# Delta-rule chain in full 128x128 matmuls: z computed beside y1, one block-diagonal inverse for two heads, state columns beside y2

## The chip, the cores and the metric

The kernel runs on one core of one Trainium2 chip. The metric is the device time of one execution in microseconds; of several executions the median is taken. Engines are named as the profile names them: PE (TensorE, matrix multiplication), PEld (its weight loads), DVE (VectorE), ACT (ScalarE), POOL (GpSimd) and SP (SyncE, which issues the DMAs).

## The reference, cut to what matters

The reference is one decoder block on 512 tokens of width 1024: an RMS norm, two parallel token mixers (HGRN2 with 8 heads, RWKV-7 with 16 heads of 64), a gated merge and output projection, and a gated convolutional feed-forward part. The change is in the RWKV-7 mixer, a delta rule whose state has 64 x 64 entries per head:

```
def step(state, inp):
    r_t, w_t, k_t, v_t, a_t, b_t = inp
    sa = jnp.einsum('bhvk,bhk->bhv', state, a_t)
    state = (state * w_t[:, :, None, :] + sa[..., None] * b_t[:, :, None, :]
             + v_t[..., None] * k_t[:, :, None, :])
    y = jnp.einsum('bhvk,bhk->bhv', state, r_t)
    return state, y
```

Its output y is normalised per head, scaled, joined by a bonus term and a gate, and projected.

## The kernel before, in words

**Stages.** A first phase projects the normalised input by the 66 column blocks of `w_in` (128 columns each) and runs both mixers. The second phase multiplies both mixers' outputs by `w_branch_a` and `w_branch_b` (tile `yps`, line 1223), merges, projects by `w_out`, and runs the feed-forward part. The large products are done as three float32r matmuls each (high and low parts of both operands); every weight block is loaded by SP into `raw`, its high part is cast on ACT (`whi_t`), its low part subtracted on POOL (`wlo_t`). The mixers' own products are fp32 matmuls; each fp32 matmul is two PE instructions in the trace.

**The delta rule in chunks.** The 16 heads are treated as 8 pairs (`hb`), one head in partitions 0 to 63 (`hs[0]`), the other in 64 to 127 (`hs[1]`). The 512 tokens are cut into NCH = 8 chunks of 64. For each pair there are three generators:
- `front` (line 702) prepares decayed keys and queries (`gt`, `bk`), multiplies them into the chunk's score matrices (`sc`), masks these into `lr` (strictly lower part for the inverse, lower part with diagonal for y2) and `gt`, and transposes `bk` into `bkn`. All lie in `X`, a buffer of which there are two; so front of pair hb waits for `("chain", hb - 2)` at line 746, and its first step behind that wait is `kka` (line 750).
- `solve` (line 817) inverts each chunk's unit triangular 64 x 64 matrix in blocks of 16, with two DMA round trips, into `Q` (a 64 x 64 inverse per head, each in its head's partitions).
- `chain` (line 872) steps through the 8 chunks. `sv` holds, per chunk and head, the state in the head's own partitions and the values in the other head's. A step first computes z (lines 887 to 889) and y1 (890 to 893), from `gt` and `sv`, with outputs in half of the partitions each; copies z to `zs` on DVE (895); multiplies by the inverse (902); scales the result into `sv` on DVE, once per head (905); computes the state update from `bkn` (908) and y2 from `lr` (910), which adds to y1 in PSUM (`yp`); and adds the decayed state `sp` (made on ACT, 900) into the next chunk's `sv` on DVE, once per head (918). Behind the last step stands a part that normalises `yp` (its first instruction is the reduction into `ym`, 926), transposes it and writes it out. chain of pair hb starts when solve of pair hb and all of chain of pair hb - 1 are through.

A chain step has ten matmuls (eight in the last chunk): four for z and y1, two by the inverse, two for the state, two for y2. Their stationary operands are 64 columns wide. PE forms in the profile give the array's rows and columns in use, as in `128*64`, and then the moving operand.

**The order of the work.** In the first phase every engine's instructions are put in a fixed order by a planner (class `Plan`, line 78). Generators yield one operation at a time; the planner prices each (`cost`, line 152), computes when its operands are ready (`prepare`, line 129: end of the producer plus a hop, and `MARGIN` = 0.6 us more for PE), and emits the operation that can start first, with a head start (`BONUS`) for the chain. On the chip each engine runs its list in that order. Dense products fill PE between the rest: `load`, `splits` and `gemm` (lines 1089, 1106, 1144) handle one weight block each, with gates: a block is loaded when the pair it feeds has got far enough. The blocks of the two merge gates come last: GA is let go at `("late", 6)`, GB at `("late", 7)`, which chain sets behind its sixth chunk (line 919). The second phase begins when they are done.

## Time and profile before

| | |
|---|---|
| median of 3 runs | 1256.02 us (1255.92 to 1258.85) |
| the profiled execution | 1255.5 us, its span 1253.8 us |
| granted TensorE clock over the span | 0.989 |
| PE busy | 1210.6 us (97%), 7748 matmul instructions |
| DVE, ACT, POOL busy | 732.7, 463.6, 536.0 us |
| first phase | from the start to 743.7 us |
| first chain's first z, last chain's last y2 | 153.2 us, 682.1 us |

The time of an execution is its span and what lies around it. A row of the timeline gives start, duration, engine, line, operation, output tile and input tiles, the PE form, and how many like instructions were merged; 207 is the line of the planner's `emit`, so in the first phase instructions are told apart by their tiles: `us<-sv,X` is z and the state update, `yp<-sv,X` y1 and y2, `us<-zs,Q` the product with the inverse, `zps` a dense product. Matmul durations overlap; what one costs PE is the distance from its start to the next one's.

### The profile page before, as it was taken

How to read it: one execution, taken by the hardware profiler on the slowest of the kernel's cores; microseconds unless marked ns; L12 is line 12 of the kernel's file. 1: busy time of each engine (PE TensorE's matmuls, PEld its weight loads, DVE VectorE, ACT ScalarE, POOL GpSimd, SP SyncE). 2: the span in 40 equal slices, each digit the busy share in tenths (PEclk: the TensorE clock that was granted, in tenths of full speed). 3: DMA queues.
4: the chain of work that ended last, by engine and by line, in shares of the span. 5: the costliest groups of instructions: out<-in, count | busy, mean ns of one | idle time of the engine just before them, and what ended most of it. 6: DMA issues, size and time to landing. Idle time of an engine off the chain costs nothing.

```text
span 1253.8 us, 19765 instructions
## 1 busy us (share of the span) xinstructions
PE 1210.6 (97%) x7748; PEld 949.7 (76%) x7748; DVE 732.7 (58%) x1563; ACT 463.6 (37%) x825; POOL 536.0 (43%) x420
## 2 busy tenths in 40 slices
PE   8889999999999999999999999999999999999997
PEld 6667668667668677686767888888988888888886
DVE  6988887787888988886746304335523232322213
ACT  5533334333343443343332532225534343342321
POOL 6444224342332423242424454432466575565631
PEclk9889899999999999999999999999999999999999
DMA  5121212112112122121221733254323232232332
GB/s 178 50 68 58 65 43 87 49 55 68 50 61 64 54 65 68 43 75 55 70 72 49 240 118 118 86 186 156 130 85 115 90 112 84 84 101 80 122 101 84
DMA packets 54061, 111.01 MB, mean 89 GB/s; under 512 B 21584, under 2 KB 24784, under 8 KB 53968
## 3 DMA queue, kind: packets, MB, share of 16 engines
q1 hardware_dynamic: 53968, 109.75, 27.6%
q8 instruction: 61, 1.00, 0.3%
q14 instruction: 32, 0.26, 0.1%
HBM read 100.29 MB, written 9.44 MB: 88 GB/s over the span
## 4 chain that ended last, share of the span: by engine, by line
PE 75%; DVE 15%; issue 3%; ACT 3%; POOL 2%; DMA 1%; SPq 0%; DVEq 0%; POOLq 0%; ACTq 0%
PE zps L207 20%; PE zps L323 6%; PE zps L322 6%; PE zps L321 6%; PE dn L321 3%; PE dn L323 3%; PE dn L322 3%; PE us L207 3%; PE sc L207 2%; PE yps L321 2%; PE yps L323 2%; PE yps L322 2%; PE vps L207 2%; PE mix L207 2%; DVE X L207 2%
## 5 line engine op out<-in xcount | busy, mean ns | idle before, releaser
L207 POOL TENSOR_TENSOR wlo_t<-raw,whi_t 128x512 fp32r<-128x512 f32 x134 | 184.6, 1397 | 351.3 <-ACT whi_t L207 319.8
L279 POOL TENSOR_TENSOR wlo_t<-raw,whi_t 128x1024 fp32r<-128x1024 f32 x80 | 194.6, 2439 | 96.4 <-ACT whi_t L279 96.2
L207 PE MATMUL zps<-xl,whi_t 128*128 128x512 f32 x488 | 201.3, 413 | 0.0
L207 PE MATMUL zps<-xh,wlo_t 128*128 128x512 f32 x488 | 201.2, 412 | 0.0
L207 PE MATMUL zps<-xh,whi_t 128*128 128x512 f32 x488 | 200.6, 411 | 0.0
L279 ACT CAST whi_t<-raw 128x1024 fp32r<-128x1024 f32 x80 | 83.3, 1049 | 175.5 <-DMA raw<-wup 64.5
L1378 DVE SCALAR_TENSOR_TENSOR u<-zps,pr,u 128x511 f32<-128x511 f32 x40 | 30.0, 750 | 190.7 <-ACT u L1377 190.7
L207 ACT CAST whi_t<-raw 128x1024 fp32r<-128x1024 f32 x71 | 74.4, 1048 | 147.1 <-PE zps L207 68.1
L321 PE MATMUL zps<-x2h,whi_t 128*128 128x512 f32 x320 | 125.5, 392 | 0.0
L323 PE MATMUL zps<-x2h,wlo_t 128*128 128x512 f32 x320 | 125.5, 392 | 0.0
L322 PE MATMUL zps<-x2l,whi_t 128*128 128x512 f32 x320 | 125.5, 392 | 0.0
L207 PEld LDWEIGHTS zps<-xl,whi_t 128*128 128x128 f32 x488 | 92.5, 190 | 20.6 <-issue 0.5
L207 PEld LDWEIGHTS zps<-xh,wlo_t 128*128 128x128 f32 x488 | 92.7, 190 | 20.1 <-issue 0.2
L207 PEld LDWEIGHTS zps<-xh,whi_t 128*128 128x128 f32 x488 | 92.8, 190 | 19.4 <-issue 0.2
L321 PEld LDWEIGHTS zps<-x2h,whi_t 128*128 128x128 f32 x320 | 60.2, 188 | 13.5
L322 PEld LDWEIGHTS zps<-x2l,whi_t 128*128 128x128 f32 x320 | 60.2, 188 | 13.5
L323 PEld LDWEIGHTS zps<-x2h,wlo_t 128*128 128x128 f32 x320 | 60.1, 188 | 13.4
L1403 POOL TENSOR_TENSOR th<-th,u 128x512 f32<-128x512 f32 x22 | 28.4, 1292 | 71.2 <-DVE u L1379 71.2
L207 ACT ACTIVATE sp<-sv,pel 64x64 f32<-64x64 f32 x96 | 33.0, 344 | 67.0 <-DVE sv L207 65.8
L207 PEld LDWEIGHTS us<-sv,X 128*64 128x64 f32 (+1 forms) x480 | 23.8, 134 | 39.7 <-issue 11.6
L207 DVE TENSOR_SCALAR sv<-us,rn 64x64 f32<-64x64 f32 x128 | 35.8, 280 | 29.0 <-PE us L207 25.3
L321 PE MATMUL yps<-oh,whi_t 128*128 128x512 f32 x128 | 50.2, 392 | 0.0
(375 smaller groups left out, 2601.0 us busy)
## 6 DMA issues: line engine op xcount, KB each, us to landing
raw<-win SPq DMA_DIRECT2D x64, 512.0 KB, 3.7
raw<-wup SPq DMA_DIRECT2D x44, 512.0 KB, 3.5
raw<-wdn SPq DMA_DIRECT2D x22, 512.0 KB, 3.5
raw<-wbr SPq DMA_DIRECT2D x16, 512.0 KB, 3.4
raw<-whi SPq DMA_DIRECT2D x8, 512.0 KB, 3.5
raw<-wout SPq DMA_DIRECT2D x8, 512.0 KB, 3.5
xt<-xT SPq DMA_DIRECT2D x8, 256.0 KB, 6.4
oa_d<-hg SPq DMA_DIRECT2D x8, 256.0 KB, 2.2
```

What stands on the lines that cost most here:

```text
L207: op.ins_ = self.seq(op.key, op.fn(*op.args, **op.kw))
L279: return A.copy(hi, raw), eng.tensor_tensor(lo, raw, hi.bitcast(F32), op=ALU.subtract)
L321: T.matmul(o, lh, rh, start=start, stop=False)
L322: T.matmul(o, lh, rl, start=False, stop=False)
L323: T.matmul(o, ll, rh, start=False, stop=stop)
L1378: V.scalar_tensor_tensor(u[:, 1:S], ps[:, 0 : S - 1], pc("cw1", b), u[:, 1:S], op0=ALU.mult, op1=ALU.add)
L1403: G.tensor_tensor(th, th, uv_, op=ALU.mult)
```

## The change

- **z beside y1.** `gt` holds both operands side by side, so one matmul with 128 stationary columns per head gives z in one half of the output's partitions and y1 in the other. In chunk 0 it now runs over all 128 rows, and the empty half of `sv` is zeroed on POOL.
- **One inverse for both heads.** Two tiles `qd` (128 x 128 per chunk, zeroed once each) hold the two inverses as diagonal blocks; a single matmul serves both heads. `solve` still works in a tile `Q` (now one buffer) and copies the halves into `qd` on ACT.
- **State columns beside y2.** `lr` and `bkn` become `w2`: per chunk and head 128 columns, of which the head's own 64 hold `bkn` and the other 64 the y2 scores in the head's rows. In the other head's rows these 64 columns first hold the strictly lower part for `solve`, which zeroes them on POOL when it is through. One matmul per head gives the state update and y2, in the last chunk too.
- **y.** y1 and y2 no longer add up in PSUM. ACT copies each, per head and chunk, into `ys` and `yb`; DVE adds the two once per pair. z goes to `zs` half on DVE, half on ACT, and of the two scalings of `sv` one goes to ACT.
- **PSUM.** Five 64-column slots per step wander through 16 slots in two banks (`ua`, `ub`).
- **Room and planner.** `sgx` has one buffer, `f2` is gone (the scan of `p2` runs in place), `fm` uses `Tn`, `qs` overwrites `qi`. The planner prices a matmul of 64 moving by 128 stationary columns at 0.112 us.

Per chain step: matmuls ten to five, all in the form 128*128; DVE copies, scalings and additions five to four; ACT operations two to eight.

```
+            elif n == 64 and m == 128:
+                op.us = 0.112
...
+    qds = [mx.tile([P, NCH, P], F32, name=f"qd{i}") for i in range(2)]
...
-        lr = X[:, 4 * S : 6 * S].rearrange("p (n x c) -> p n x c", n=NCH, x=2)
-        bkn = X[:, 6 * S : 8 * S].rearrange("p (n c) -> p n c", n=NCH)
+        w2 = X[:, 4 * S : 8 * S].rearrange("p (n h c) -> p n h c", n=NCH, h=2)
...
-                yield V1.tensor_tensor(lr[q, n0 : n0 + 4, h], sc[q, :, h], mr[q, n0 : n0 + 4], op=ALU.mult)
-                yield V1.tensor_tensor(lr[q, n0 : n0 + 4, 1 - h], sc[q, :, 1 - h],
+                yield V1.tensor_tensor(w2[q, n0 : n0 + 4, 1 - h, hs[h]], sc[q, :, h], mr[q, n0 : n0 + 4], op=ALU.mult)
+                yield V1.tensor_tensor(w2[q, n0 : n0 + 4, h, hs[1 - h]], sc[q, :, 1 - h],
...
-            yield A1.copy(bkn[:, 4 * half : 4 * half + 4], tp)
+            dst = w2[:, 4 * half : 4 * half + 4].rearrange("p n h c -> p n (h c)")
+            dst = bass.AP(dst.tensor, dst.offset, [list(dst.ap[0]), [2 * P, 4], [P + 64, 2], [1, 64]])
+            yield A1.copy(dst, tp.rearrange("p n (h c) -> p n h c", h=2))
...
-        Q = mx.tile([P, NCH, 64], F32, name="Q", bufs=2)
+        Q = mx.tile([P, NCH, 64], F32, name="Q")
+        qd = qds[hb % 2]
+        if hb < 2:
+            yield G1.memset(qd, 0.0)
...
-        fm = mx.tile([P, NCH, 64], F32, name="fm")
+        fm = Tn
...
         yield V1.tensor_tensor(Q, Q, dps, op=ALU.add)
+        for h in range(2):
+            yield A1.copy(qd[hs[h], :, hs[h]], Q[hs[h]])
...
-            yield A1.copy(Q[a, :, 32:64], dps2[a])
+            yield A1.copy(qd[a, :, 64 * h + 32 : 64 * h + 64], dps2[a])
+        for h in range(2):
+            yield G1.memset(w2[hs[h], :, 1 - h, hs[h]], 0.0)
...
         sv = mx.tile([P, NCH, 2, 64], F32, name="sv")
+        for h in range(2):
+            yield G1.memset(sv[hs[h], 0, h], 0.0)
...
-        yp = pyz.tile([P, NCH, 64], F32, name="yp")
-        us = pus.tile([P, 8, 64], F32, name="us", tag="us")
+        ua = pus.tile([P, 8, 64], F32, name="us", tag="us")
+        ub = pyz.tile([P, 8, 64], F32, name="yp")
+        ys = mx.tile([P, NCH, 64], F32, name="ys")
+        yb = mx.tile([P, NCH, 64], F32, name="yb")
+
+        def slot(i):
+            return (ua if i % 16 < 8 else ub)[:, i % 8]
+
         for n in range(NCH):
-            zslot, uslot, sslot = (3 * n) % 8, (3 * n + 1) % 8, (3 * n + 2) % 8
-            for h in (1, 0):
-                kp = slice(0, P) if n > 0 else hs[1 - h]
-                yield T1.matmul(us[hs[h], zslot], gt[kp, n, h, h], sv[kp, n, h], start=True, stop=True)
-            for h in (1, 0):
-                kp = slice(0, P) if n > 0 else hs[1 - h]
-                yield T1.matmul(yp[hs[1 - h], n], gt[kp, n, h, 1 - h], sv[kp, n, h], start=True, stop=False,
-                                skip_group_check=True)
+            zy, us, sy = [slot(5 * n), slot(5 * n + 1)], slot(5 * n + 2), [slot(5 * n + 3), slot(5 * n + 4)]
+            for h in range(2):
+                yield T1.matmul(zy[h], gt[:, n, h].rearrange("p x c -> p (x c)"), sv[:, n, h], start=True, stop=True)
             zs = small.tile([P, 64], F32, name="zs")
-            yield V1.tensor_copy(zs, us[:, zslot])
+            yield V1.tensor_copy(zs[hs[0]], zy[0][hs[0]])
+            yield A1.copy(zs[hs[1]], zy[1][hs[1]])
...
-            for h in (1, 0):
-                yield T1.matmul(us[hs[h], uslot], Q[hs[h], n], zs[hs[h]], start=True, stop=True)
             for h in range(2):
-                q = hs[h]
-                yield V1.tensor_scalar(sv[q, n, h], us[q, uslot], rn2[q, n : n + 1], None, op0=ALU.mult)
-            if n < NCH - 1:
-                for h in (1, 0):
-                    yield T1.matmul(us[hs[h], sslot], bkn[:, n, hs[h]], sv[:, n, h], start=True, stop=True)
-            for h in (1, 0):
-                yield T1.matmul(yp[hs[1 - h], n], lr[hs[h], n, 1 - h], sv[hs[h], n, h], start=False, stop=True,
-                                skip_group_check=True)
+                yield A1.copy(ys[hs[1 - h], n], zy[h][hs[1 - h]])
+            yield T1.matmul(us, qd[:, n], zs, start=True, stop=True)
+            yield V1.tensor_scalar(sv[hs[0], n, 0], us[hs[0]], rn2[hs[0], n : n + 1], None, op0=ALU.mult)
+            yield A1.activation(sv[hs[1], n, 1], us[hs[1]], AF.Identity, scale=rn2[hs[1], n : n + 1])
+            for h in range(2):
+                yield T1.matmul(sy[h], w2[:, n, h], sv[:, n, h], start=True, stop=True)
             if n < NCH - 1:
...
+            for h in range(2):
+                yield A1.copy(yb[hs[1 - h], n], sy[h][hs[1 - h]])
...
-        ys = mx.tile([P, NCH, 64], F32, name="ys")
+        yield V1.tensor_tensor(ys, ys, yb, op=ALU.add)
...
-        yield V1.tensor_tensor_scan(p2.rearrange("p a n c -> p (a n c)"), f2.rearrange("p a n c -> p (a n c)"),
+        yield V1.tensor_tensor_scan(p2.rearrange("p a n c -> p (a n c)"), p2.rearrange("p a n c -> p (a n c)"),
```

More of the change, by code (lines that the diff above doesn't have):

```diff
@@ L391, in block_kernel @@
     Gi.memset(mh, 1.0)
-    sgx = [pers.tile([P, NCH, 65], F32, name=f"sgx{i}") for i in range(2)]
+    sgx = pers.tile([P, NCH, 65], F32, name="sgx")
     m65 = pers.tile([P, NCH, 65], F32, name="m65")
@@ L400, in block_kernel @@
     scm = pers.tile([P, NT, P], F32, name="scm")
-    for t_ in sgx:
-        Gi.memset(t_[:, :, 0:1], 0.0)
-    Gi.memset(f2[:, :, :, 0:1], 0.0)
+    Gi.memset(sgx[:, :, 0:1], 0.0)
     Gi.memset(scm, 0.0)
@@ L715, in front @@
         yield T1.matmul(wps, lw[:, 0:P], zws, start=False, stop=True)
-        sg = sgx[hb % 2]
+        sg = sgx
         yield A1.activation(sg[:, :, 1:65], c8(wps), AF.Tanh, scale=0.5, bias=hw0[:, hb : hb + 1])
@@ L796, in front @@
                 yield D1.dma_start(lb_d[:, h, b].rearrange("n s t -> s n t"),
-                                   lr[p0 : p0 + 16, :, h, 16 * b : 16 * b + 16])
-        st_[hb] = [vt[hb], gt, lr, bkn, pel, rn2]
+                                   w2[p0 : p0 + 16, :, 1 - h, p0 : p0 + 16])
+        st_[hb] = [vt[hb], gt, w2, pel, rn2]
         fin.add(("lb", hb))
-        plan.spawn("solve", solve(hb, lb_d, lr))
+        plan.spawn("solve", solve(hb, lb_d, w2))
         bks = bk.rearrange("p n x c -> p n (x c)")
@@ L813, in front, with solve @@
                 yield T1.transpose(tp[:, n], bks[:, 4 * half + n], ident)
-            yield A1.copy(bkn[:, 4 * half : 4 * half + 4], tp)
+            dst = w2[:, 4 * half : 4 * half + 4].rearrange("p n h c -> p n (h c)")
+            dst = bass.AP(dst.tensor, dst.offset, [list(dst.ap[0]), [2 * P, 4], [P + 64, 2], [1, 64]])
+            yield A1.copy(dst, tp.rearrange("p n (h c) -> p n h c", h=2))
         fin.add(("front", hb))
-    def solve(hb, lb_d, lr):
+    def solve(hb, lb_d, w2):
         if hb > 0:
@@ L841, in solve @@
             for h in range(2):
-                yield T1.matmul(fps[hs[h], n], lr[hs[h], n, h], Tn[hs[h], n], start=True, stop=True)
-        fm = mx.tile([P, NCH, 64], F32, name="fm")
+                yield T1.matmul(fps[hs[h], n], w2[hs[h], n, 1 - h, hs[h]], Tn[hs[h], n], start=True, stop=True)
+        fm = Tn
         yield V1.tensor_tensor(fm, fps, mf.unsqueeze(1).broadcast_to([P, NCH, 64]), op=ALU.mult)
@@ L855, in solve @@
             for n in range(NCH):
-                yield T1.matmul(fps2[b, n], lr[a, n, h, 32:64], Tn[a, n, 0:32], start=True, stop=True)
+                yield T1.matmul(fps2[b, n], w2[a, n, 1 - h, b], Tn[a, n, 0:32], start=True, stop=True)
         for h in range(2):
@@ L866, in solve @@
             a = slice(64 * h, 64 * h + 32)
-            yield A1.copy(Q[a, :, 32:64], dps2[a])
+            yield A1.copy(qd[a, :, 64 * h + 32 : 64 * h + 64], dps2[a])
+        for h in range(2):
+            yield G1.memset(w2[hs[h], :, 1 - h, hs[h]], 0.0)
         yield done(("front", hb))
-        st_[hb].append(Q)
+        st_[hb].append(qd)
         fin.add(("solve", hb))
     def chain(hb):
-        v, gt, lr, bkn, pel, rn2, bo, Q = st_.pop(hb)
+        v, gt, w2, pel, rn2, bo, qd = st_.pop(hb)
         sv = mx.tile([P, NCH, 2, 64], F32, name="sv")
+        for h in range(2):
+            yield G1.memset(sv[hs[h], 0, h], 0.0)
         vp = pus.tile([P, NT, P], F32, name="vp", tag="us")
@@ L915, in chain @@
                     if n == 0:
-                        yield V1.tensor_copy(sv[q, 1, h], us[q, sslot])
+                        yield V1.tensor_copy(sv[q, 1, h], sy[h][q])
                     else:
-                        yield V1.tensor_tensor(sv[q, n + 1, h], us[q, sslot], sp[h][q], op=ALU.add)
+                        yield V1.tensor_tensor(sv[q, n + 1, h], sy[h][q], sp[h][q], op=ALU.add)
+            for h in range(2):
+                yield A1.copy(yb[hs[1 - h], n], sy[h][hs[1 - h]])
             if n == NCH - 3:
@@ L923, in chain @@
         yield D1.dma_start(lgr, wlg[hb, :, 2 * P : 3 * P])
-        ys = mx.tile([P, NCH, 64], F32, name="ys")
+        yield V1.tensor_tensor(ys, ys, yb, op=ALU.add)
         ym = small.tile([P, NCH], F32, name="ym")
-        yield V1.tensor_reduce(ym, yp, axis=AX.X, op=ALU.add)
+        yield V1.tensor_reduce(ym, ys, axis=AX.X, op=ALU.add)
         yield V1.tensor_single_scalar(ym, ym, 1.0 / 64, op=ALU.mult)
-        yield V1.tensor_tensor(ys, yp, ym.unsqueeze(2).broadcast_to([P, NCH, 64]), op=ALU.subtract)
-        yield A1.activation(yp, ys, AF.Square)
+        yield V1.tensor_tensor(ys, ys, ym.unsqueeze(2).broadcast_to([P, NCH, 64]), op=ALU.subtract)
+        yield A1.activation(yb, ys, AF.Square)
         yss = small.tile([P, NCH], F32, name="yss")
-        yield V1.tensor_reduce(yss, yp, axis=AX.X, op=ALU.add)
+        yield V1.tensor_reduce(yss, yb, axis=AX.X, op=ALU.add)
         yield from rsq1(yss, NCH, 64 * GN_EPS)
@@ L1041, in hgrn @@
             yield T1.matmul(ups[:, t], k3[:, t], vn[:, t, hv], start=True, stop=True)
-        qs = mx.tile([P, 16, 32], F32, name="qs")
-        yield V1.tensor_tensor(qs, qi[:, 0:16], cq.rearrange("p t j -> p (t j)").unsqueeze(2).broadcast_to([P, 16, 32]),
+        qs = qi[:, 0:16]
+        yield V1.tensor_tensor(qs, qs, cq.rearrange("p t j -> p (t j)").unsqueeze(2).broadcast_to([P, 16, 32]),
                                op=ALU.mult)
```

8 lines of the change are left out of this document (4 added, 4 removed).

## The prediction

> **What bounds the kernel now.** I read the page first, then the windows of the first phase, the DVE timeline around the hand-over between head pairs, and the PE timeline around the chain.
>
> ```profile
> PE 1210.6 (97%) x7748; PEld 949.7 (76%) x7748; DVE 732.7 (58%) x1563; ACT 463.6 (37%) x825; POOL 536.0 (43%) x420
> ```
> ```profile
> 400.00:500.00 100.00, 96.75 (x867) 72.41 (x866) 88.34 (x206) 40.26 (x88) 35.54 (x32) 1.00 0.23 68
> 685.00:743.40 58.40, 58.40 (x256) 47.11 (x255) 13.60 (x13) 26.28 (x35) 30.07 (x23) 1.00 0.53 173
> ```
> The columns of the second view are busy us of PE, PEld, DVE, ACT and POOL. Between 400 and 500 us the chain runs and PE is busy for 97 of 100 us, DVE for 88; ACT has 60 us to spare. From 685 to 743 us only dense matmuls are left and PE is full. So PE time removed from the phase should come off the end, if the order of the work lets the dense matmuls move forward. That order hangs on a loop: front of pair hb+2 waits for the chain of pair hb, solve for front, chain for solve.
>
> ```profile
> 319.45 0.75 DVE L207 SCALAR_TENSOR_TENSOR v<-zps,pr,v 128x511 f32<-128x511 f32 x1
> ...
> 338.26 0.69 DVE L207 TENSOR_REDUCE ym<-yp 128x8 f32<-128x512 f32 x1
> ...
> 339.81 0.68 DVE L207 SCALAR_TENSOR_TENSOR kka<-ta,k 128x512 f32<-128x512 f32 x1
> ```
> ```profile
> 539.67 0.68 DVE L207 TENSOR_REDUCE ym<-yp 128x8 f32<-128x512 f32 x1
> ...
> 548.61 0.75 DVE L207 SCALAR_TENSOR_TENSOR v<-zps,pr,v 128x511 f32<-128x511 f32 x1
> 549.27 0.68 DVE L207 SCALAR_TENSOR_TENSOR kka<-ta,k 128x512 f32<-128x512 f32 x1
> ```
> The first ym after a chain marks its end; kka is the first step of the next front that had to wait. At pair 4 v was ready 19 us before, and kka starts 1.5 us after chain 2 ended: the loop sets the pace. At pair 7 chain 5 ended at 539.7, but kka waits for v, which came out of a dense matmul, until 549.3: there PE sets the pace, and 9.6 us of the odd pairs' loop are PE's.
>
> ```profile
> 671.30 0.47 DVE L207 TENSOR_TENSOR sv<-us,sp 64x64 f32<-64x64 f32 x2 [0.71 <-PE us L207]
> ```
> ```profile
> 698.88 0.40 PE L207 MATMUL zps<-xh,whi_t 128*128 128x512 f32 x1
> ...
> 743.68 0.39 PE L321 MATMUL yps<-oh,whi_t 128*128 128x512 f32 x1
> ```
> ```profile
> raw<-win SPq DMA_DIRECT2D x64, 512.0 KB, 3.7
> ```
> ```profile
> L207 POOL TENSOR_TENSOR wlo_t<-raw,whi_t 128x512 fp32r<-128x512 f32 x134 | 184.6, 1397 | 351.3 <-ACT whi_t L207 319.8
> ...
> L207 ACT CAST whi_t<-raw 128x1024 fp32r<-128x1024 f32 x71 | 74.4, 1048 | 147.1 <-PE zps L207 68.1
> ```
> The last eight blocks (GB) are let go when chain 7 has added its sixth state, at 671.3. Their weights would need 3.7 us to land, 1.0 for the cast and 2.8 for the split, so they could start near 679; the first starts at 698.9, because GA blocks still stand in the queue. These 20 us are PE's too. Phase 1 ends when yps begins, at 743.7.
>
> **The change, part by part.** PE first. The chain's matmuls of before use half or a quarter of the array, and each excursion from the dense matmuls can be read off the PE timeline:
>
> ```profile
> 502.12 0.40 PE L207 MATMUL zps<-xl,whi_t 128*128 128x512 f32 x1
> 502.45 0.34 PE L207 MATMUL us<-sv,X 128*64 128x64 f32 x4
> 502.71 0.33 PE L207 MATMUL yp<-sv,X 64*64 64x64 f32 x4
> 502.97 0.50 PE L207 MATMUL zps<-xh,wlo_t 128*128 128x512 f32 x1
> 503.31 0.39 PE L207 MATMUL zps<-xh,whi_t 128*128 128x512 f32 x1
> 503.54 0.40 PE L207 MATMUL zps<-xl,whi_t 128*128 128x512 f32 x1
> ...
> 504.25 0.40 PE L207 MATMUL zps<-xl,whi_t 128*128 128x512 f32 x1
> 504.57 0.34 PE L207 MATMUL us<-sv,X 128*64 128x64 f32 x4
> 504.74 0.29 PE L207 MATMUL yp<-sv,X 128*64 128x64 f32 x4
> 504.96 0.50 PE L207 MATMUL zps<-xh,wlo_t 128*128 128x512 f32 x1
> 505.29 0.39 PE L207 MATMUL zps<-xh,whi_t 128*128 128x512 f32 x1
> ```
> ```profile
> 262.65 0.40 PE L207 MATMUL zps<-xh,whi_t 128*128 128x512 f32 x1
> 262.98 0.33 PE L207 MATMUL us<-zs,Q 64*64 64x64 f32 x4
> 263.24 0.50 PE L207 MATMUL zps<-xl,whi_t 128*128 128x512 f32 x1
> 263.57 0.39 PE L207 MATMUL zps<-xh,wlo_t 128*128 128x512 f32 x1
> ```
> One fp32 matmul is two instructions. Dense ones start 0.23 us apart (503.31 to 503.54). Around an excursion the dense one ahead takes 0.32 to 0.33 and the one behind 0.34: 0.20 us are lost to leaving and returning. The state update with y2 costs 503.31 - 502.12 - 2 x 0.23 = 0.73 us, z with y1 505.29 - 504.25 - 0.46 = 0.58, the inverse 263.57 - 262.65 - 0.46 = 0.46: together 1.77 us a step where each stands alone. Without the 0.20 each they are 0.52 + 0.39 + 0.26 = 1.17.
>
> After, a step has five matmuls, ten instructions, all 128x128 with 64 moving columns, a form the trace doesn't show. It lies between these two:
>
> ```profile
> 252.28 1.05 PE L207 MATMUL nps<-blk,sq 128*128 128x2 f32 x8
> 253.20 0.48 PE L207 MATMUL zps<-xh,wlo_t 128*128 128x512 f32 x1
> ```
> ```profile
> 304.08 0.94 PE L207 MATMUL ups<-vn,k 128*128 128x128 f32 x6
> 304.77 0.48 PE L207 MATMUL zps<-xh,whi_t 128*128 128x512 f32 x1
> ```
> With 2 moving columns eight take 0.92 us, with 128 six take 0.69: 0.115 each in both, a few ns of it the return from tiles. Since 2 and 128 columns cost the same, 64 do, and I take 0.112: 1.12 us a step. (The new planner cost of 0.112 for a whole matmul is half of that.)
>
> ```profile
> L207 PE MATMUL us<-sv,X 128*64 128x64 f32 (+1 forms) x480 | 40.3, 246 | 5.5 <-DVE sv L207 5.4
> L207 PE MATMUL yp<-sv,X 64*64 64x64 f32 (+1 forms) x512 | 39.9, 234 | 0.0
> ...
> L207 PE MATMUL us<-zs,Q 64*64 64x64 f32 x256 | 21.3, 242 | 2.5 <-DVE zs L207 2.5
> ```
> So 1248 instructions become 640. Walking the PE timeline, the 1248 stand in 195 groups, 155 of them (79%) with 128x128 work on both sides; the rest border on sc, hsc or solve, which keep their switches. The saving is 1.17 - 1.12 + 0.79 x 0.60 = 0.52 us a step, 64 steps 33 us, less 8 x 0.27 for the last steps, which had no state update and now compute its columns with y2: **31 us**, of which I count 30. Bounds: 2 us if all bordered on tiles, 39 if none did.
>
> [...]
>
> DVE loses one scaling of sv a step and gains the addition of y1 and y2 per pair:
>
> ```profile
> L207 DVE TENSOR_SCALAR sv<-us,rn 64x64 f32<-64x64 f32 x128 | 35.8, 280 | 29.0 <-PE us L207 25.3
> ...
> L207 ACT ACTIVATE sp<-sv,pel 64x64 f32<-64x64 f32 x96 | 33.0, 344 | 67.0 <-DVE sv L207 65.8
> ...
> L207 ACT COPY sv<-vp 64x256 f32<-64x256 f32 x32 | 11.7, 367 | 8.3 <-PE vp L207 7.7
> ```
> 64 x 0.28 = 18 us off, 8 x 0.69 (as ym) = 5.5 on. The zs copy keeps its time at half its rows; the other in-place edits (fm, qs, p2, sg) cost nothing on DVE, their old readers being done earlier in the same generator. ACT gains six operations a step: half of zs, two of y1, head 1's scaling, two of y2. Each lies below 0.37 us (a copy four times as wide, from PSUM) and I put the copies near 0.21, that row less 192 elements at the cast's 1.0 ns: five copies and one sp-like 0.34, 1.4 us a step, 90 us in all (upper bound 2.2 us, 140). Over the eight chains, some 530 us, that is 17 to 26% of ACT's time: the 40% of 400 to 500 us would become 57 to 66, no bound by throughput. Two copies of half a qd per solve (512 columns, half a cast each) run beside DVE's transpose of Q and put nothing on the path. POOL gains memsets of parts of w2, sv, qd and p2, at most 1.4 us for each large one (the split's row, twice as many rows); two stand at the end of each solve, where chain's first use of w2 comes only after the v transposes, z and u; a late one would cost a split's 2.8 us once per pair.
>
> The chain's own step. Two full matmuls end later than two tiled ones: four of ups would take 0.94 - 2 x 0.115 - 0.10 = 0.6 us against 0.34, twice a step, but head 0's addition starts after the first of them, so +0.27 once; u +0.05; the two scalings side by side -0.28; an excursion's entry no longer paid, 0.10 three times. That is about -0.2 before ACT is asked. New is that head 1's half of zs and of sv wait in ACT's queue, at worst behind a 1.05 us cast each time; ACT being 40 to 57% busy I take half of 1.05 for each step's two together, net **+0.3 us** a step (range -0.2 to +1.9). Queued behind such a wait on ACT are casts and the zps evacuations, on which POOL's splits wait; these have 20 us of queued blocks as cover.
>
> Sum against the profiled execution, 1255.5 us (span 1253.8 and 1.7 around it). PE allows -30. The loop of odd pairs allows: 20 us of queued GA blocks, plus 9.6 at pair 7's v, less 0.3 x 32 steps (chains 1, 3, 5, 7) = -20. The later of the two counts: -20 to -22, with DVE's 12 us making it a little less tight: 1233.5, and 1234 on the scale of the median, which is 0.5 higher.
>
> **Rivals.** *ACT sets the chain* (slower): each step waits for whole casts twice. The loop turns the gain into a loss when the step grows by 30/32 = 0.94 us; at +1.3 the end is 32 x 1.3 - 30 = 12 later: 1268. For it: ACT's in-order queue and a planner that prices the new matmuls at half. Against: ACT idles 60%. 12%. *The gain is used up*: step +0.8 to +1.0, 1252 to 1259, 8%. *Packing wins* (slower): no switch is saved and five tiled pairs at 0.17 = 0.85 us become 1.12: 64 x 0.27 = 17, PE being full: 1273. Against: 155 of 195 groups. 4%. *Both shorten*: the step stays or shrinks, PE's 30 come off: 1219 to 1227, 20%.
>
> **Numbers.** The forecast with its neighbours (1227 to 1251) has 56%. A difference of 0.3% (3.8 us) is what a measurement of this kernel can tell. Faster 0.76, same 0.08, slower 0.16. The range 1220 to 1258 leaves out the two slower rivals and the tip of the fastest.
>
> **What would show it.** The dense matmul ahead of chain work 0.23 us before it, not 0.33; 640 chain instructions, 0.112 us apart inside a group; ACT busy 57% in mid-phase; yps starting near 722; kka at pair 7 right after ym. A step of the loop is wrong if a chain of eight steps has become longer by more than 3 us, and the forecast with it if by more than 7; the price of the new matmul is wrong if they start 0.05 or 0.2 us apart; the whole is wrong if yps starts after 743 with PE idle ahead of chain matmuls whose operand ACT wrote.

## The result, and the profile after

The changed kernel takes 1292.05 us (median of 4 runs, 1288.63 to 1295.42) where the kernel before takes 1256.41 us on the same chip (median of 4): a ratio of 1.028, 95% interval 1.0248 to 1.0311. It is slower by some 36 us; the forecast was 1234. The profiled execution has a span of 1288.9 us. The first line of its page:

```profile
PE 1222.0 (95%) x7140; PEld 986.3 (77%) x7140; DVE 723.4 (56%) x1507; ACT 554.7 (43%) x1225; POOL 551.5 (43%) x460
```

There are 608 matmul instructions fewer, and PE is busy 11 us longer. The second phase did not change (510.1 us from the first `yps` to the span's end before, 510.6 after), so all of the loss lies in the first. The windows from 100 us to the first `yps`, of before and then of after (length; busy us of PE, PEld, DVE, ACT and POOL; granted PE clock; DMA share; GB/s):

```profile
100.00:743.80 643.80, 624.36 (x5074) 468.06 (x5073) 483.83 (x1223) 241.15 (x511) 229.70 (x201) 0.99 0.24 71
```
```profile
100.00:778.50 678.50, 633.98 (x4465) 503.10 (x4464) 473.69 (x1167) 332.47 (x911) 245.55 (x242) 0.96 0.23 68
```
```profile
400.00:500.00 100.00, 94.66 (x665) 74.78 (x664) 78.64 (x201) 53.17 (x151) 37.41 (x38) 0.97 0.20 57
600.00:700.00 100.00, 87.01 (x611) 68.37 (x611) 59.14 (x171) 46.24 (x145) 26.50 (x27) 0.88 0.21 61
```

PE idles 44.5 us of the stretch where it idled 19.4, and its mean clock over it is 0.96 in place of 0.99. DVE has 10 us less (12 were forecast). ACT is busy for 53 of the 100 us from 400 to 500 (57 were forecast). No engine is full; PE least of all between 600 and 700 us, where before it was busy for 97.2 of the 100.

The price of the new matmuls is as forecast. The PE timeline of after:

```profile
264.16 0.39 PE L209 MATMUL zps<-xl,whi_t 128*128 128x512 f32 x1
264.39 0.33 PE L209 MATMUL us<-zs,qd 128*128 128x64 f32 x2
264.53 0.48 PE L209 MATMUL zps<-xh,wlo_t 128*128 128x512 f32 x1
264.85 0.40 PE L209 MATMUL zps<-xh,whi_t 128*128 128x512 f32 x1
...
265.79 0.40 PE L209 MATMUL zps<-xl,whi_t 128*128 128x512 f32 x1
266.02 0.55 PE L209 MATMUL us<-sv,X 128*128 128x64 f32 x4
266.38 0.48 PE L209 MATMUL zps<-xh,wlo_t 128*128 128x512 f32 x1
266.70 0.39 PE L209 MATMUL zps<-xh,whi_t 128*128 128x512 f32 x1
```

By the prediction's own sum, two instructions cost 264.85 - 264.16 - 0.46 = 0.23 us and four cost 266.70 - 265.79 - 0.46 = 0.45, so a step costs 0.23 + 2 x 0.45 = 1.13 us (1.12 forecast, 1.77 before), and the dense matmul ahead takes 0.23, not 0.33. By these prices some 30 us of PE work are gone, and the end came later all the same. The busy time rose although the work fell: PE ran at half its clock for 41 us longer than before (47.8 us for 6.8, last section). That is some 20 us of busy time, an estimate from these numbers and from the dense matmuls, which away from other PE work start 0.42 to 0.43 us apart in after's stretches of half clock and 0.23 outside them; the rest of the rise was not traced.

Where the time was lost shows at the ends of the chains (the reduction into `ym`). Chain 6 of before, chain 6 and the pair-7 hand-over of after, then the first `yps` of after:

```profile
607.40 0.69 DVE L207 TENSOR_REDUCE ym<-yp 128x8 f32<-128x512 f32 x1
```
```profile
564.84 0.67 DVE L209 SCALAR_TENSOR_TENSOR kka<-ta,k 128x512 f32<-128x512 f32 x1
...
568.27 0.69 DVE L209 TENSOR_REDUCE ym<-ys 128x8 f32<-128x512 f32 x1
...
644.10 0.69 DVE L209 TENSOR_REDUCE ym<-ys 128x8 f32<-128x512 f32 x1
```
```profile
778.29 0.39 PE L323 MATMUL yps<-oh,whi_t 128*128 128x512 f32 x1
```

Chain 6 ends 36.7 us later, and `yps` follows it by 134.2 us (136.3 before). In the 20 kernels of this study that distance is 126 to 140 us: behind the sixth step of chain 6 GA is let go, and from there PE works off a nearly fixed rest. So the end follows chain 6, to within some 7 us. At pair 7 `kka` no longer waits for `v`: it starts 3.4 us ahead of `ym`, where before it came 9.6 us behind. That part of the forecast came true, and was lost elsewhere. The way to chain 6's end, added up from the first `kka` of pair 2 over the pairs 2, 4 and 6 (front: `kka` to the first `nb`; solve: to the first transposition of `v`; chain: to `ym`; gaps: `ym` to the next `kka`), in us, with three kernels of the experiments below:

| | pair 2's kka | fronts | solves | chains | gaps | chain 6 ends |
|---|---|---|---|---|---|---|
| before | 201.1 | 129.4 | 119.6 | 146.8 | 10.4 | 607.4 |
| after | 195.3 | 139.1 | 135.4 | 167.1 | 7.2 | 644.1 |
| x0_room | 196.5 | 135.6 | 132.6 | 156.4 | 4.5 | 625.7 |
| n1_banks | 194.3 | 137.3 | 135.9 | 157.8 | 7.2 | 632.5 |
| r2_qcopy | 195.0 | 120.5 | 137.0 | 155.6 | 9.5 | 617.6 |

The chains became 20 us longer, the solves 16, the fronts 10. Of the chains' 20 us, 9.8 lie between the first and the last copy of z to `zs` (126.5 us before, 136.3 after), 4.5 ahead of the first, and 6.0 behind the last, where y1 and y2 must now be copied out and added ahead of `ym`.

A new wait stands in the chain's way. The waits of PE between 150 and 700 us (total, times, longest), before and after:

```profile
PE us L207 <- DVE sv L207: 5.4, 7, 1.8
PE yt L207 <- DVE ys L207: 2.8, 2, 1.8
PE us L207 <- DVE zs L207: 2.5, 5, 0.8
```
```profile
PE us L209 <- ACT ys L209: 8.5, 14, 1.6
PE yp L209 <- ACT ys L209: 6.2, 9, 2.2
PE us L209 <- ACT yb L209: 4.1, 4, 1.8
PE us L209 <- ACT sv L209: 4.0, 8, 0.9
...
PE yp L209 <- ACT yb L209: 3.4, 6, 1.2
```

PE waits 22.2 us for the copies of y (`ys`, `yb`), though no chain matmul reads them. The timeline of one step of after, all engines:

```profile
309.61 0.22 DVE L209 COPY zs<-yp 64x64 f32<-64x64 f32 x1 [0.56 <-PE yp L209]
...
309.86 0.21 ACT L209 COPY zs<-yp 64x64 f32<-64x64 f32 x1 [1.30 <-DVE zs L209]
...
310.07 0.70 ACT L209 ACTIVATE sp<-sv,pel 64x64 f32<-64x64 f32 x2
...
310.69 0.41 ACT L209 COPY ys<-yp 64x64 f32<-64x64 f32 x2
...
311.15 0.43 PE L209 MATMUL yp<-zs,qd 128*128 128x64 f32 x2 [0.20 <-ACT ys L209]
...
311.62 0.28 DVE L209 TENSOR_SCALAR sv<-yp,rn 64x64 f32<-64x64 f32 x1 [0.53 <-PE yp L209]
```

`zs` is complete at 310.07. The matmul that reads it starts at 311.15, the moment ACT's second y copy ends, and in ACT's queue the two `sp` stand ahead of those copies. (Dense matmuls fill most of that time on PE, which idles only 0.20 us; the chain's next result is late all the same.) All three, z, the y columns and u, lie in one PSUM bank here (`yp`). The slots let one kernel show both cases: from the end of `zs` to u takes 1.09 us on average in the first six steps of a chain, where u shares a bank with at least one y copy, and 0.50 in the seventh, where it does not.

The same wait orders the readers: ACT's half of `zs` starts when DVE's half ends, not beside it. Both halves go to one tile, so that could be the reason instead of the bank. The fourth step of each chain tells, where slots 15 and 16 put the two z results into different banks:

```profile
683.09 0.21 ACT L209 COPY zs<-us 64x64 f32<-64x64 f32 x1 [0.26 <-PE us L209]
...
685.38 0.21 DVE L209 COPY zs<-yp 64x64 f32<-64x64 f32 x1
...
685.62 0.21 ACT L209 COPY ys<-yp 64x64 f32<-64x64 f32 x1 [1.61 <-DVE zs L209]
```

ACT's half starts 2.3 us ahead of DVE's, and it is the y copy, into another tile but out of DVE's bank, that waits for DVE. In none of the eight fourth steps did ACT's half wait for DVE's; in 48 of the 56 others it did. So in this program an access by one engine to a PSUM bank waits for another engine's access to the same bank, whatever columns the two touch: of the 631 accesses to `us` and `yp` by DVE and ACT in after, from 149 to 713 us, none overlaps one by the other engine to the same bank. (Each of the two banks is one tile here, so the runs don't tell bank from tile.) The row of u agrees (it waits to 311.15, 1.08 us after `zs` is complete, for a read of other columns); the halves of `zs` lie in different partitions, 0 to 63 and 64 to 127, and yet they wait (ACT's starts at 309.86, DVE's ends at 309.83).

### The profile page after: what moved, and what is told of

Same layout as the page of the kernel before. It is cut to its first block, busy times and chain, and to the rows that moved or that the text cites. A ratio compares the mean times of both kernels' runs of the same rounds, so it can differ in the third digit from the quotient of the medians.

```text
span 1288.9 us, 19123 instructions
## 1 busy us (share of the span) xinstructions
PE 1222.0 (95%) x7140; PEld 986.3 (77%) x7140; DVE 723.4 (56%) x1507; ACT 554.7 (43%) x1225; POOL 551.5 (43%) x460
## 4 chain that ended last, share of the span: by engine, by line
PE 56%; DVE 7%; ACT 3%; POOL 1%; DMA 1%; issue 1%; DVEq 0%; POOLq 0%; ACTq 0%; SPq 0%
PE zps L209 11%; PE zps L323 6%; PE zps L324 6%; PE zps L325 6%; PE dn L323 3%; PE dn L324 3%; PE dn L325 3%; PE yps L323 2%; PE yps L324 2%; PE yps L325 2%; PE us L209 2%; PE yp L209 2%; PE sc L209 1%; DVE ys L209 1%; PE vps L209 1%
## 5 line engine op out<-in xcount | busy, mean ns | idle before, releaser
L209 PEld LDWEIGHTS us<-sv,X 128*128 128x128 f32 x288 | 43.1, 198 | 23.4 <-ACT yb L209 9.2
L209 PE MATMUL us<-sv,X 128*128 128x64 f32 x288 | 48.7, 282 | 9.5 <-ACT yb L209 4.1
L325 PE MATMUL yps<-oh,wlo_t 128*128 128x512 f32 x128 | 50.2, 392 | 0.0
```

Source lines behind the costliest of these rows:

```text
L209: op.ins_ = self.seq(op.key, op.fn(*op.args, **op.kw))
L325: T.matmul(o, ll, rh, start=False, stop=stop)
```

## The experiments

Two theories stood at the start. **Queue**: ACT's new work (y copies, halves of z and u) lengthens the chain. **Room**: what the change does to make space (solve's copies, shared buffers, w2) lengthens front and solve. The rival to both was that PE's saved time is simply not on the path (**loop**).

**x6_dve_no_y.** After, with `zs` and both scalings on DVE, and y left out (ACT makes no y copies, `ys` is zeroed).
```
-            yield A1.copy(zs[hs[1]], zy[1][hs[1]])
+            yield V1.tensor_copy(zs[hs[1]], zy[1][hs[1]])
...
-            for h in range(2):
-                yield A1.copy(ys[hs[1 - h], n], zy[h][hs[1 - h]])
...
+            yield V1.tensor_scalar(sv[hs[1], n, 1], us[hs[1]], rn2[hs[1], n : n + 1], None, op0=ALU.mult)
```


> The changed kernel with ACT kept out of the chain step: all of zs and both scalings on DVE, and y1 and y2 not copied out at all (y is left out: ys is zeroed). What is left is the change of the matmuls. Theory (the extra ACT operations lengthen front, solve and chain by their place in ACT's queue): 1225 to 1245, so faster than before, because PE's 30 us come off. Rival (the full-width matmuls themselves make the chain later, or the planner's low price puts things in a bad order): 1275 or more.

Measured: 1281.76 us, ratio 1.0192 (1.0153 to 1.023). Ten us of 36 go with ACT's part in the step; most stays. PE's waits for the y copies are gone here, but those for DVE's `sv` are 18.3 us (5.4 before), so this run does not price the copies alone.

**x4_before_copies.** The kernel before with four ACT copies of 64x64 out of `yp` added to each step.
```
+            for h in range(2):
+                yield A1.copy(ys[hs[1 - h], n], yp[hs[1 - h], n])
```


> The kernel before with four ACT copies of 64 x 64 per chain step added (y1 as it stands in PSUM, both heads, before the inverse; y after y2, both heads), results unused. Theory (ACT's queue): 1275 to 1295, 20 to 40 us slower than before, with front and solve each 3 to 5 us longer. Rival (full-width matmuls or their price): within 8 us of before.

Measured: 1258.08 us, ratio 0.9999 (0.9981 to 1.0017). 256 copies more on ACT cost nothing. Here u goes to another bank (`us`) than the one that is copied out of, which at this point I had not seen. As a matter of ACT's load, the queue theory falls.

**x0_room.** After with the old tiled chain (its matmuls, `zs`, scalings and y in PSUM as before), on `w2`, `qd` and all the room edits, but without the zeroings in `w2` and `sv`, which the old chain doesn't need.
```
+                yield T1.matmul(us[hs[h], zslot], gt[kp, n, h, h], sv[kp, n, h], start=True, stop=True)
...
+            yield V1.tensor_copy(zs, us[:, zslot])
...
+                yield T1.matmul(us[hs[h], uslot], qd[hs[h], n, hs[h]], zs[hs[h]], start=True, stop=True)
...
+                    yield T1.matmul(us[hs[h], sslot], w2[:, n, h, hs[h]], sv[:, n, h], start=True, stop=True)
```

> The changed kernel with the old chain: tiled matmuls, y summed in PSUM, zs and both scalings on DVE, but with all that made room (one sgx, no f2, one Q, fm in Tn, qs in qi, w2 for lr and bkn) and the inverse copied into the diagonal tile. Theory (ACT in the chain): within 8 us of before. Rival (the room taken away, or the two extra copies in solve, cost the time): 1270 or more.

Measured: 1277.93 us, ratio 1.0154 (1.0116 to 1.0192). The room edits, without one full matmul, cost 20 us: more than half of the loss.

**x5_inverse.** x0 with one full matmul for both inverses.
```
-            for h in (1, 0):
-                yield T1.matmul(us[hs[h], uslot], qd[hs[h], n, hs[h]], zs[hs[h]], start=True, stop=True)
+            yield T1.matmul(us[:, uslot], qd[:, n], zs, start=True, stop=True)
```


> As the control with the old chain in the new room, but one full matmul for both heads' inverse; z, y1, state and y2 stay tiled. One excursion of 0.46 us less 0.22 is saved per step, 64 x 0.24 x 0.79 = 12 us of PE, and no ACT operation is added to the step. Theory (ACT's queue is what costs): 5 to 12 us faster than before, 1244 to 1251. Rival (the form of the matmul costs): as slow as its share of the change, 1265 to 1270.

Measured: 1268.91 us, ratio 1.0088 (1.0057 to 1.0119). Of the three merged products this one, which brings no new copy per step, gives back some 8 us.

**r5_w2, r1_p2, r3_share, r2_qcopy.** The room edits put one by one into the kernel before: `w2` for `lr` and `bkn`; the scan in place; one `sgx`, `fm` in `Tn`, `qs` in `qi`; and, on top of the last, solve's result copied out of `Q` by ACT:
```
-        lr = X[:, 4 * S : 6 * S].rearrange("p (n x c) -> p n x c", n=NCH, x=2)
-        bkn = X[:, 6 * S : 8 * S].rearrange("p (n c) -> p n c", n=NCH)
+        w2 = X[:, 4 * S : 8 * S].rearrange("p (n h c) -> p n h c", n=NCH, h=2)
```
```
-        yield V1.tensor_tensor_scan(p2.rearrange("p a n c -> p (a n c)"), f2.rearrange("p a n c -> p (a n c)"),
+        yield V1.tensor_tensor_scan(p2.rearrange("p a n c -> p (a n c)"), p2.rearrange("p a n c -> p (a n c)"),
```
```
-        fm = mx.tile([P, NCH, 64], F32, name="fm")
+        fm = Tn
```
```
+        for h in range(2):
+            yield A1.copy(Q2[hs[h]], Q[hs[h]])
```


> The kernel before with one part of the change: lr and bkn become w2, with bkn's columns between those of the scores. The planner takes a strided operand as the box around it, so the copies of bkn, the DMA reads of the scores and solve's matmuls now seem to touch the same columns. Theory of the layout: 8 to 20 us slower than before, with solve later against front. Theory of solve's copies or of the shared buffers: within 4 us of before.

> The kernel before with one part of the change: f2 gone, the scan of p2 in place, a memset of its gaps on POOL ahead of each hgrn. Theory of the layout: within 4 us of before. Theory that hgrn now starts behind POOL's splits: 5 to 15 us slower, hgrn's first DVE operation later by up to 2.8 us in each pair.

> The kernel before with one part of the change: one sgx, fm in Tn, qs in qi. Theory of the layout: within 4 us of before. Theory that the shared buffers tie solve or hgrn to earlier readers: 5 to 15 us slower.

> As the run with the shared buffers, and in solve one Q, whose halves are copied on ACT into a second tile that the chain reads (64 columns wide, so the chain's matmuls stay as before). Theory of solve's copies: 5 to 15 us slower than the run without them, the stretch from the first dps matmul to the second transpose longer by 1 to 3 us (it is 3.5 before, 6.2 after). Theory of the layout: within 4 us of that run.

Measured: 1.0004 (0.9991 to 1.0018), 1.0013 (0.9997 to 1.0029), 1.0002 (0.998 to 1.0024), and 1.0071 (1.0048 to 1.0093; 1267.0 us). Only the two copies cost, 8.5 us. By the table above the solves of pairs 2, 4 and 6 are 17 us longer than before, the chains 9 longer and the fronts 9 shorter. In r5 every engine runs the same instructions in the same order as before, so the layout of `w2` costs nothing by itself. How the copies might cost, the timelines of pair 4 suggest, first of before, then of after:

```profile
420.54 0.67 DVE L207 TENSOR_TENSOR Q<-Q,dps 128x512 f32<-128x512 f32 x1
...
421.47 0.69 DVE L207 STREAM_TRANSPOSE Tn<-Q 128x512 f32<-128x512 f32 x1
```
```profile
427.52 0.67 DVE L209 TENSOR_TENSOR Q<-Q,dps 128x512 f32<-128x512 f32 x1
428.29 1.26 ACT L209 COPY qd<-Q 64x512 f32<-64x512 f32 x2 [0.26 <-DVE Q L209]
...
431.44 0.70 DVE L209 STREAM_TRANSPOSE Tn<-Q 128x512 f32<-128x512 f32 x1
```

The transposition does not need the copies. But solve yields one operation at a time, so the planner is offered the transposition only once it has placed both copies behind what ACT has to do, and fills DVE with other work meanwhile: 3.3 us from Q's end to the transposition, 0.3 before. In r2 itself, however, this distance is only 0.97 us on average of the eight pairs, where before has 0.58.

**s1_late and s3_inverse_late.** To test that reading, both copies are yielded behind the `fps2` matmuls, in after (s1) and in x5 (s3).
```
-        for h in range(2):
-            yield A1.copy(qd[hs[h], :, hs[h]], Q[hs[h]])
         yield V1.transpose(Tn.rearrange("p n c -> p (n c)"), Q.rearrange("p n c -> p (n c)"))
...
                 yield T1.matmul(fps2[b, n], w2[a, n, 1 - h, b], Tn[a, n, 0:32], start=True, stop=True)
+        for h in range(2):
+            yield A1.copy(qd[hs[h], :, hs[h]], Q[hs[h]])
```


> The changed kernel with one move: solve's two copies of Q's halves into the diagonal tile are yielded behind the sixteen fps2 matmuls, not ahead of the second transpose. The planner holds one operation per generator, so ahead of the transpose they keep it from DVE's list until ACT has a place for both. Theory of the yield order: 6 to 12 us faster than the changed kernel, 1280 to 1286, the stretch from the first dps matmul to the second transpose back from 6.2 to about 4. Rival (the copies cost by ACT's time): no change, 1288 to 1295.

> The run with one matmul for both inverses and all else tiled (1268.9), with the same move of solve's copies. Theory of the yield order: 6 to 12 us faster than that run, 1257 to 1263, so about as before. Rival (ACT's time): 1266 to 1270.

Measured: 1300.26 us, 1.0341 (1.0305 to 1.0376), and 1267.95 us, 1.01 (1.0069 to 1.0131). The first is 8 us slower than after, the second as x5. The distance did get shorter, on average from 2.3 to 1.1 us in s1 and from 1.7 to 1.0 in s3, and the time did not fall. So this delay is not what the copies cost by; the reading falls as an explanation, though the rows stand.

**x7_order and x1_price.** After with the y copies yielded later (`ys` behind the state matmuls, `yb` in the next step), and after without the planner's new price (0.218 us for the new matmul instead of 0.112).
```
+            if n > 0:
+                for h in range(2):
+                    yield A1.copy(yb[hs[1 - h], n - 1], psy[h][hs[1 - h]])
...
-            for h in range(2):
-                yield A1.copy(yb[hs[1 - h], n], sy[h][hs[1 - h]])
```
```
-            elif n == 64 and m == 128:
-                op.us = 0.112
```

> The changed kernel with one move: the copies of y1 are yielded behind the step's last matmuls and those of y2 behind the next step's inverse, so that no y copy stands ahead of a critical matmul in the generator. Theory of the yield order: the planned place of the inverse and of the next z no longer waits for ACT, the chain step shrinks by 0.2 to 0.5 us, 6 to 15 us faster than the changed kernel. Rival (the step's length is that of its own operations, as the full matmuls end later): within 5 us of it.

> The changed kernel with the planner's price of the new matmul at 0.218 us in place of 0.112 (measured: 2 x 0.112). Theory of the yield order and of the loop's length: within 6 us of the changed kernel. Rival (the low price puts chain operations too early in DVE's and ACT's lists, which then wait for PE): 10 to 25 us faster.

Measured: 1287.96 us, 1.0243 (1.0212 to 1.0275), and 1284.3 us, 1.022 (1.0198 to 1.0241). They give 4 us (not clear of noise) and 8 us; neither accounts for the loss. In x7 the chain's matmuls no longer wait for `ys` or `yb`, but all the engines' lists are in another order than in after, so it does not price those waits.

**g1_no_y2.** The kernel before without its y2 matmuls: PE relief alone.
```
...
-            for h in (1, 0):
-                yield T1.matmul(yp[hs[1 - h], n], lr[hs[h], n, 1 - h], sv[hs[h], n, h], start=False, stop=True,
-                                skip_group_check=True)
```


> The kernel before with the two y2 matmuls of each chain step left out (its y lacks the term that adds the step's own v); nothing else is changed. That takes 128 matmuls, 256 instructions of 64x64, 17 us of PE by the step's 0.27 us for them, off the loop, and no wait, copy or buffer is added. If the chain, front and solve of a pair in a row set the pace and PE is only busy beside them (loop theory), the time falls by at most 5 us (1252 to 1258) and the saved PE time shows as idle PE. If PE sets the pace before the change (the prediction's step a, its saving of 30 us reaching the end), it falls by 12 to 17 us (1240 to 1245).

Measured: 1258.81 us, ratio 1.0001 (0.9977 to 1.0025). The window from 100 us to its first `yps`:

```profile
100.00:745.70 645.70, 616.10 (x4821) 462.54 (x4820) 487.21 (x1224) 241.25 (x511) 230.36 (x201) 0.98 0.23 71
```

PE is busy 8 us less than before and idles 29.6 us where it idled 19.4; the end stays. That is what the loop theory expected: some 17 us of PE work were taken out, nothing was added, and the time did not fall. It does not show why. Chain 6 ended 8.7 us later than before (`ym` at 616.1), and the rest behind it was 6.8 us shorter (129.5 us to `yps`, 136.3 before), so the saving may have come through in that rest and been lost ahead of it. The planner put the lists in another order, and PE ran at half its clock for 31 us (7 before); the runs don't separate the two.

**j1_idle_work.** After with two matmuls of the identity ahead of u's in u's slot.
```
+            for _ in range(2):
+                yield T1.matmul(us, ident, ident[:, 0:64], start=True, stop=True)
             yield T1.matmul(us, qd[:, n], zs, start=True, stop=True)
```


> The kernel after with two matmuls of the identity into the slot of u ahead of u's own matmul in each chain step: four instructions of 0.112 us, 0.45 us a step, 28.7 us of PE work that waits for nothing but the slot. Loop theory: PE has 90 us of stalls between 100 and 700 us, so a good part of it goes into them, and the time rises by 0 to 12 us (1290 to 1304); if half-clock stretches are what the stalls cost, those (48 us of them) get fewer and the time may even fall by up to 15 us. If PE still sets the pace after the change, the time rises by 25 to 29 us (1317 to 1321).

Measured: 1370.51 us, ratio 1.0898 (1.0877 to 1.092): 78 us for 29 us of PE work. Both theories missed, and it says nothing of idle PE or of the clock, since the added matmuls wait themselves. (PE idled 43.6 us between 100 and 700 us in after, not the 90 of the expectation.) PE's waits:

```profile
PE us L209 <- ACT ys L209: 26.4, 32, 3.3
PE yp L209 <- ACT ys L209: 9.6, 13, 2.0
```

They write the bank that ACT copies y out of, so they wait for the copies, and everything behind them in PE's queue with them. This row is what led to the bank.

**v1_inverse_pool and c1_three.** x5 with solve's copies on POOL; after with the old price, the later y copies and solve's copies on POOL together.
```
-            yield A1.copy(qd[hs[h], :, hs[h]], Q[hs[h]])
+            yield G1.tensor_copy(qd[hs[h], :, hs[h]], Q[hs[h]])
```


> The kernel x5 (old tiled chain but one full matmul for both inverses, 1.0088 of the time before) with the two copies of half an inverse in each solve on GpSimd and not on ScalarE. If those copies cost because they stand in ScalarE's queue ahead of solve's next copies (4.77 to 6.24 us from dps to the second transpose in x5 and after, 3.5 before), that piece returns to near 3.5 to 4.5 us and the time falls by 4 to 10 us, to 0.999 to 1.005 of before. If they cost because they hold Q longer wherever they run, or GpSimd is slow at them (over 1 us each), the time stays at 1.007 to 1.015.

> The kernel after with three of its scheduling choices put otherwise at once: the planner's old price for the 128x64 matmul (0.218, worth 8 us alone), the y copies yielded later (4 us alone), and the inverse's two copies on GpSimd. If the lengthening comes of how the steps are put on the engines, the three add up and it runs at 1268 to 1278 (1.009 to 1.017). If each only shifts the interleaving by chance, they don't add, and it stays at 1280 to 1290. Neither theory has it below the kernel before.

Measured: 1269.77 us, 1.009 (1.0066 to 1.0115), and 1287.44 us, 1.0233 (1.0209 to 1.0257). On POOL the copies cost what they cost on ACT. The three do not add up: together they are no faster than the price alone. The likely reading, with s1, is that a rearrangement by the planner moves the time by some 8 us either way; steps of that size in a run with another order are not put down to a mechanism here.

**n1_banks.** After, with z and y1 always in one bank, u and the state columns always in the other.
```
-            zy, us, sy = [slot(5 * n), slot(5 * n + 1)], slot(5 * n + 2), [slot(5 * n + 3), slot(5 * n + 4)]
+            zy, us = [ua[:, (2 * n + h) % 8] for h in range(2)], ub[:, (3 * n) % 8]
+            sy = [ub[:, (3 * n + 1 + h) % 8] for h in range(2)]
```


> The kernel after with the slots of the chain's results laid out by bank: both z results always in the one PSUM bank, u and both state results always in the other; after counts its slots through both banks, so that in most steps u lands in the bank that ScalarE copies y1 out of. In after's trace u's matmul starts at the end of ScalarE's y copies (311.15 us, the second copy ends at 311.10) though its operand zs was ready at 310.06, and PE's waits for those copies are 22 us between 150 and 700 us. Bank theory: these waits leave the list (under 5 us), the chain from its first to its last z gets 1 to 2 us a pair shorter (42.7 to 43.7 where after has 44.75), and of 22 us half lies in the loop: 1278 to 1286. Rival (the chain's length does not set the end, or the planned distance of some 1 us between zs and u hides the copies): within 4 us of after, 1288 to 1296.

Measured: 1275.21 us, ratio 1.0138 (1.0114 to 1.0163): 17 us faster than after, more than expected. In the two traces every engine runs the same instructions in the same order (7140 on PE, 1507 on DVE, 1225 on ACT, 460 on POOL), so no rearrangement by the planner stands beside the bank here. PE's waits and the like step of its timeline:

```profile
PE yp L209 <- ACT sv L209: 10.3, 14, 1.9
PE yp L209 <- ACT zs L209: 7.3, 8, 1.7
PE yt L209 <- DVE ys L209: 3.8, 5, 1.4
```
```profile
307.91 0.21 ACT L209 COPY zs<-us 64x64 f32<-64x64 f32 x1 [0.77 <-DVE zs L209]
...
308.14 0.72 ACT L209 ACTIVATE sp<-sv,pel 64x64 f32<-64x64 f32 x2
...
308.59 0.33 PE L209 MATMUL yp<-zs,qd 128*128 128x64 f32 x2
...
308.77 0.41 ACT L209 COPY ys<-us 64x64 f32<-64x64 f32 x2
```

The waits for `ys` and `yb` are gone from the list; u starts 0.47 us after `zs` is complete (308.12) and ahead of the y copies, where in the step shown of after it started 1.08 later and behind them. Over the first seven steps of the chains the mean is 0.67 where after has 1.00. From its first to its last copy of z the chain takes 42.5 us a pair (after 44.6, before 42.7). Bank theory holds. The halves of `zs` still follow each other here, and PE now waits 17.6 us for ACT's halves of `sv` and `zs`, which its matmuls do read. The chains of pairs 2, 4 and 6 remain 11 us longer than before in the table, but not in their steps (127.5 us from the first to the last copy of z, 126.5 before): 3.9 us lie ahead of the first and 6.1 behind the last. In x0, whose chains are 10 us longer, 7 lie in the steps, so the two rests are not the same loss.

**n2_banks_zero.** n1, with POOL's zeroing of `w2` started as soon as solve has read the blocks for the last time.
```
+        plan.spawn("solve", zero(hb, w2))
...
-        for h in range(2):
-            yield G1.memset(w2[hs[h], :, 1 - h, hs[h]], 0.0)
+        yield done(("zero", hb))
```


> n1_banks, and GpSimd's two zeroings of the blocks in w2 start as soon as the second product of the inverse has read them, beside solve's last steps, and not behind its last copy. If the wait for GpSimd is what makes solve's end late (4.89 us from the last matmul to the chain's first transpose in x0, 3.11 before), 2 to 8 us less than n1_banks; if GpSimd has them done in time anyway, within 4 us of n1_banks. At or below the kernel before (ratio 1.000) only if the room that the full matmuls need costs nothing but these zeroings and waits, which the runs of x0 and r2 speak against.

Measured: 1277.56 us, ratio 1.0157 (1.0133 to 1.0181), as n1. POOL's zeroing was in time, as far as a run with another order of the lists can tell.

So of the 36 us, 17 are the shared bank (after less n1). The other 18 or so, which n1 keeps, are not traced to the end. The room edits are the main suspect, since x0 loses 20 us by them without one full matmul; but x0's lists are in another order, and its loss lies in part elsewhere than n1's. Solve's two copies cost 8.5 us when put alone into the kernel before (r2); none of the others that were tried alone costs anything clear of noise, and the way in which those copies lengthen the solves is open. The 30 us of PE that the full matmuls save show nowhere on balance: n1 has them, x0 has not, and both stand at 1.014 to 1.015. That they are worth nothing by themselves is not shown: x5, with one merged product and no copy more than x0, is 8 us faster than x0, and in n1 a gain may be hidden behind the new waits for ACT. No kernel here beats the one before.

## Why the prediction was wrong

- **The step that failed** is the sum: "The loop of odd pairs allows: 20 us of queued GA blocks, plus 9.6 at pair 7's v, less 0.3 x 32 steps (chains 1, 3, 5, 7) = -20", taken as what PE's 30 us then turn into. It holds fronts and solves at their old length, prices the chains' growth at 10 us, and takes a full PE for a PE that the end waits for. In its place the runs showed that the fronts and solves of pairs 2, 4 and 6 grew by 25 us and their chains by 20, so that chain 6 ended 36.7 us later; that 17 us of the loss are waits for a shared PSUM bank (n1), a term the sum doesn't have; and that some 17 us of PE work taken out alone brought nothing (g1). Why the fronts and solves grew stays open beyond the 8.5 us of solve's copies.
- **The pace.** "the loop sets the pace" was right and should have been carried through: it was chain 6's end that moved `yps`, through the even pairs. `yps` near 722 was forecast, 778.3 came, with PE idle ahead of chain matmuls that wait for ACT: close to the case named as "the whole is wrong", though the copies that they mostly wait for are not their operands.
- **Price of the matmuls and the switches:** right (1.13 us a step for 1.12, saving near 30). *Packing wins* is refuted with it: its 0.17 us is the distance from 504.57 to 504.74 in the prediction's rows, four tiled instructions, and what such tiles gain they lost again in the 0.20 us around an excursion: 1.77 us a step before, 1.13 after. The lower bound of the saving, 2 us, comes to 1 by the prediction's own figures; nothing hangs on it.
- **ACT.** Right as a load (53% for 57), and x4 shows that the copies cost nothing by number. The price of 0.21 us a copy does not come out of its working (0.367 less 192 x 1.0 ns is 0.175), but 0.21 is what a copy took: luck. Wrong in putting "nothing on the path" for solve's two copies: r2 gives 8.5 us for them.
- **The chain's step.** +0.3 us forecast; from its first to its last copy of z a chain of eight steps became 1.9 us longer (42.7 to 44.6), 0.28 for each of seven steps. So +0.3 was the right size, by luck, since the reason was wrong: not a cast ahead of `zs` and `sv` in ACT's queue but y copies in the bank that u is written to. And the price was wrong: 0.3 us x 32 steps were counted as 10 us, and removing the bank's part in n1, which brings the chain back to 42.5, gave 17. Of these, chain 6 ends 11.6 us sooner (632.5 for 644.1), and 4.2 come off the rest behind it.
- **DVE:** -12 forecast, -10 in the windows. **POOL:** its zeroing hidden as forecast, as far as n2 shows.
- **The rivals.** *ACT sets the chain* had the right sign and the right engine, at 1268 and 12%, with the wrong mechanism: no whole casts were needed and the step did not grow by 1.3. The measured time lay above the range; the room edits, which the prediction had mostly put at nothing, were never a rival of their own, and x0 alone (1278) lies outside it.

## What to carry to other kernels

When a merged result is read in parts by different engines, lay it out by PSUM bank, so that no late reader (a copy that nobody waits for) shares a bank with the next result on the critical path: n1, which changed nothing but the layout by bank, was 17 us faster than after. The profile showed the shared bank as PE waiting for operations whose output it doesn't read (22.2 us for `ys` and `yb` in after). A PE that is busy for 97% of the time need not be the bound, if a chain of latencies decides when its last work may start (g1: some 17 us of PE work less, ratio 1.0001): leave some PE work out and look at the end before restructuring to save PE time. When a planner orders the work, compare the engines' lists of the two runs first; two runs with the same lists (after and n1) tell more than two without. And price the room that a change needs, each copy and each shared buffer, as a change of its own.

## What the runs showed of the hardware

- PE ran at half its clock (granted 0.5) in stretches of 3.4 us or multiples of it (in after 3.4, 6.8 and once 23.9, from 614.8 us; in before one of 6.8, from 133.8). Most followed a stall: ahead of four of the six in after between 100 us and the last few, PE idled 1.4 to 2.2 of the 3.4 us just before, and 2.5 ahead of the one in before; ahead of the one at 550.0 in after it idled 0.8, ahead of the one at 587.5 not at all. Past 100 us, without the last few us of the span, they add up to 6.8 us before, 47.8 in after (the 0.88 in the window from 600 to 700 us), 17 in x4 and 51 in n1. n1 is 17 us faster than after with as many, and x4 not slower than before with more, so they don't order the kernels. What they cost was not separated; j1 was to do it and failed. What sets them off is not shown.
- Fp32 matmuls of 128 stationary columns with 64 moving ones cost 0.113 to 0.115 us an instruction (0.45 us for four, 0.23 for two); those with 2 and with 128 cost 0.115 in the prediction's rows.
